# Retention queries decayed on GpSimd token tile by token tile, the group norm in two halves, and another turn count for the loads of w_out

## The chip, the cores and the metric

The kernel runs on one core of a Trainium2 chip. The metric is the device time of one execution in microseconds, and less is better. The core has five engines, each of which works through its own queue of instructions in order: TensorE (PE in the profile, with its weight loads as PEld), VectorE (DVE), ScalarE (ACT), GpSimd (POOL) and SyncE (SP, which here only issues transfers). An instruction waits at the head of its queue until the semaphores that it needs are set, and everything behind it on that engine waits too. TensorE has a granted clock: 1.00 in the profile is 2.4 GHz, 0.50 is 1.2 GHz.

## The reference

One transformer block over 1024 latent tokens and 256 context tokens, width 1024. The part that the change touches is the second head group, eight retention heads of width 64, in chunks of 128 tokens, run forward and backward:

```
inner = (q_c k_c^T) * decay_mat                       # within the chunk
o     = inner v_c + (q_c state) * q_decay             # q_decay: one factor per token of the chunk and head
state = state * chunk_decay + (k_c * k_decay)^T v_c   # k_decay: the same, for keys
ret   = group_norm(o_forward + o_backward) * silu(gate)   # mean and variance over the 64 of a head
out   = concat(attention, ret) @ w_out
```

The first head group is softmax attention (eight query heads, two key heads). A norm, a residual and a SwiGLU feed-forward follow. All data are fp32.

## The kernel before

The program has four stretches: the input projection, the mixing stage (attention and retention together), the output projection with `w_out`, and the feed-forward. The change lies in the mixing stage, from about 345 to 745 us of the trace.

**How the mixing stage is written.** Three Python generators are woven into one program. `attention()` walks over four pairs of heads `r`, two halves of 512 queries, ten key tiles and two heads: 160 steps, each of two score matmuls (L631, L632), an exponential on ACT (`p`, L633), four steps later two matmuls that weigh the values (`o`, L640), and the running sum `acc` of the exponentials on DVE or POOL (L688). `front(h)` finds the row maxima of the scores for head `h`: 24 score matmuls (L595), each of which DVE must read out with a maximum (`mx`, L596) before its PSUM bank is free. `retain(r)` does retention for a pair of heads:

- `U`: for each of ten token tiles the key tile is decayed on POOL (`decayed`, L737, tile `qk2`) and multiplied with the values (L751).
- The natural key and query tiles are transposed on TensorE to `kT`, `qT` (L768), copied from PSUM by ACT (L769).
- The decayed queries `q2T` are made from `qT` by DVE (forward direction) and POOL (backward direction), L774: per pair of heads four instructions on each engine, with the factors of the table `QD`.
- `ss`: the scan over the chunks, 16 small instructions on DVE (L782), and copies by ACT to `St`.
- `inner` (L799, and `im` on DVE, L802) and `outer` (L811, L813) for eight tiles; `outer` reads `q2T`.
- The group norm of `o` (L834 to L846) on DVE, ACT and POOL, then the gate product `rg` on POOL and a store to DRAM (`d_r`).

**What sets the order.** `weave` gives the next turn to the generator with the smallest share of its turns done; three weaves of 40 attention steps carry two fronts and a third of all retention turns each. What is left of the last pair's retention is written after the third weave, and the fourth weave carries the attention of the last pair and `load_w_out`: 16 halves of `w_out` tiles, each loaded by SP into one of two `raw` buffers, copied to `woh` by ACT (L125), and subtracted to `wol` by DVE (L126). A scheduler that builds the program then sets the order on each engine. The tiles `woh` lie in memory that retention has used.

Of the kernel before, what the change touches and what calls it, by code (L numbers as in the profile page):

```python
# [11 lines left out]
F32 = mybir.dt.float32  # L12
F32R = mybir.dt.float32r
AF = mybir.ActivationFunctionType
ALU = mybir.AluOpType
# [15 lines left out]
HR = 8  # L31
# [76 lines left out]
def hybrid_block(ctx: ExitStack, tc, x, c, cx, c_ctx, w_mod, b_mod, g_pre_mix, g_post_mix,  # L108
# [435 lines left out]
    lgq = bc.tile([P, 4, 2], F32, name="lgq")  # L544
    for j in range(2):
        for d in range(2):
            V.tensor_copy(out=lgq[j * HD:(j + 1) * HD, :, d],
                          in_=lg[j * HD:(j + 1) * HD, d * HR:(d + 1) * HR].rearrange("p (r j) -> p r j", j=2)[:, :, j])

# [10 lines left out]
    qs2, fr = {}, {}  # L560
# [8 lines left out]
    def front(h):  # L569
# [8 lines left out]
        V.tensor_tensor(out=q3[:, :, 0:HD], in0=qs, in1=f(q3[:, :, HD:2 * HD]), op=ALU.subtract)  # L578
# [30 lines left out]
    SKEW, V_ADDS, V_END, Q_ENG = 4, (2, 4, 6, 8), (2, 4, 6, 7, 8, 9), (V, G)  # L609
# [8 lines left out]
    def bank(tag):  # L618
        return pq.tile([P, 512], F32, tag=tag, name=tag)
# [97 lines left out]
    QD = rt.tile([P, 4, 2, P], F32, name="QD")  # L717

    def decay_matrices():
# [8 lines left out]
        for r in range(4):  # L728
            for d in range(2):
                S.activation(out=QD[:, r, d, :], in_=dcs[:, C_PR + d * P:C_PR + (d + 1) * P], func=AF.Exp, scale=lgq[:, r, d:d + 1])  # L730

    def retain(r):
        qn, kn, vn, gn = ret_load(r)

        def decayed(t):
            y = rt.tile([P, 2, 2, HD], F32, tag="qk2", name="qk2", bufs=3)
            G.tensor_tensor(out=y, in0=h3(kn[:, t, :]).unsqueeze(2).broadcast_to([P, 2, 2, HD]),  # L737
                            in1=dk[:, 1, 4 * r:4 * r + 4].rearrange("p (j d) -> p j d", d=2).unsqueeze(3).broadcast_to([P, 2, 2, HD]),
                            op=ALU.mult)
            return y  # L740
# [17 lines left out]
        if r == 0:  # L758
            decay_matrices()
# [3 lines left out]
        for nat, tr in ((kn, kT), (qn, qT)):  # L763
            for b in range(2):
# [5 lines left out]
                if nat is qn:  # L770
                    for j in range(2):
                        jsl = slice(j * HD, (j + 1) * HD)
                        for d in range(2):
# [60 lines left out]
        V.tensor_reduce(out=mu, in_=o4, axis=AX.X, op=ALU.add)  # L834
        V.tensor_scalar(out=mu, in0=mu, scalar1=1.0 / HD, scalar2=None, op0=ALU.mult)
        V.tensor_tensor(out=o4, in0=o4, in1=mu.unsqueeze(2).broadcast_to([P, nst, HD]), op=ALU.subtract)
        yield
        sq = rt.tile([P, nst, HD], F32, tag="kT", name="gsq")
        S.activation(out=sq, in_=o4, func=AF.Square)
        V.tensor_reduce(out=vr, in_=sq, axis=AX.X, op=ALU.add)  # L840
        V.tensor_scalar(out=vr, in0=vr, scalar1=1.0 / HD, scalar2=EPS, op0=ALU.mult, op1=ALU.add)
        for k in range(2):
            G.tensor_tensor(out=rs[:, k * 8:(k + 1) * 8], in0=vr[:, k * 8:(k + 1) * 8], in1=mhalf, op=ALU.pow)
        yield
        V.tensor_tensor(out=o4, in0=o4, in1=rs.unsqueeze(2).broadcast_to([P, nst, HD]), op=ALU.mult)
        G.tensor_tensor(out=gn, in0=o.rearrange("p t j e -> p t (j e)"), in1=gn, op=ALU.mult)  # L846
# [3 lines left out]
    N_FR, N_RT, N_AT = 13, 38, 40  # L850
# [29 lines left out]
    weave((islice(attend, N_AT), N_AT), (load_w_out(), 17))  # L880
# [401 lines left out]
```

## Time and profile before

| | |
|---|---|
| three runs | 1531.69, 1534.27, 1535.69 us; median 1534.27 |
| the profiled execution | 1534.52 us, of which the span from first to last instruction is 1532.7 |
| busy in the span | PE 1447.2, PEld 1083.8, DVE 866.4, ACT 518.6, POOL 501.7 us |
| mean granted clock of TensorE | 0.951 |
| mixing stage | some 400 us of the span |

Busy times are sums of the instructions of an engine. A matmul lasts about twice as long at clock 0.50, so a busy PE can still be a slow one. Idle time of an engine that nothing waits for costs nothing.

### The profile page before, as it was taken

Reading aid. Unit: us, or ns where it says so; the run is one execution under the profiler, and the core shown is the slowest. Engines: PE = TensorE matmul, PEld = TensorE weight load, DVE = VectorE, ACT = ScalarE, POOL = GpSimd, SP = SyncE. Lnnn points to the kernel's source line nnn. Section 1 sums busy time; section 2 is a strip of 40 time slices with the busy share of each in tenths; the row PEclk is TensorE's granted clock in tenths of the full one; section 3 lists DMA queues with packets and bytes.
Section 4 is the critical chain, followed back from the end, with each engine's and each line's share of the span. In section 5 each row is a group of like instructions: output and inputs, shape, how many; then the busy total and the mean of one; then the engine's idle time right before and its main releaser. Section 6 shows DMA issues by size and latency. Waiting matters only on the chain.

```text
span 1532.7 us, 19765 instructions
## 1 busy us (share of the span) xinstructions
PE 1447.2 (94%) x7290; PEld 1083.8 (71%) x7290; DVE 866.4 (57%) x1447; ACT 518.6 (34%) x1131; POOL 501.7 (33%) x382
## 2 busy tenths in 40 slices
PE   6999989998898989799899899999999999999997
PEld 2788867785454545454588678888888888888886
DVE  3667677445747676676455845444444444545445
ACT  3740221224344444545245623222222232113112
POOL 0112247303435273545003544444444441002003
PEclk9999999998676989899899999999999999999999
DMA  9456552314102020002433233222222224544662
GB/s 357 137 187 189 184 168 90 114 52 126 31 25 73 25 66 25 28 8 97 134 132 120 62 97 96 83 83 83 83 83 83 83 83 152 178 145 134 197 211 109
DMA packets 140623, 169.10 MB, mean 110 GB/s; under 512 B 8992, under 2 KB 90608, under 8 KB 140528
## 3 DMA queue, kind: packets, MB, share of 16 engines
q1 hardware_dynamic: 139680, 167.61, 33.9%
q8 instruction: 57, 0.93, 0.3%
q10 hardware_dynamic: 848, 0.25, 0.1%
q14 instruction: 38, 0.31, 0.1%
HBM read 132.17 MB, written 35.65 MB: 109 GB/s over the span
## 4 chain that ended last, share of the span: by engine, by line
PE 76%; DVE 11%; DMA 6%; issue 2%; ACT 2%; POOL 2%; SPq 0%; DVEq 0%; POOLq 0%; ACTq 0%
PE pb L131 45%; PE sb L131 14%; PE o L640 4%; PE sb L631 3%; PE sb L595 2%; DMA wm<-in_w_mod 2%; PE sb L632 2%; DVE q2T L774 1%; DMA rv<-d_p 1%; PE r L799 1%; DVE ss L782 1%; DVE mx L596 1%; PE sb L811 1%; PE r L751 1%; DVE wlo L126 1%
## 5 line engine op out<-in xcount | busy, mean ns | idle before, releaser
L131 PE MATMUL pb<-T,w 128*128 128x512 f32 x1320 | 316.7, 394 | 3.8 <-ACT w L125 2.0
L131 PEld LDWEIGHTS pb<-T,w 128*128 128x128 f32 x1320 | 247.8, 188 | 62.6 <-ACT w L125 2.6
L131 PE MATMUL pb<-whi,hT 128*128 128x512 f32 (+1 forms) x896 | 261.8, 373 | 5.2 <-ACT whi L125 4.6
L131 PEld LDWEIGHTS pb<-whi,hT 128*128 128x128 f32 x896 | 162.7, 191 | 39.3 <-ACT whi L125 5.5
L131 PE MATMUL pb<-wlo,hT 128*128 128x512 f32 (+1 forms) x448 | 165.7, 372 | 2.3 <-DVE wlo L126 2.2
L596 DVE TENSOR_REDUCE mx<-sb 128x1 f32<-128x512 f32 (+1 forms) x192 | 107.0, 596 | 62.9 <-PE sb L595 61.5
L126 DVE TENSOR_TENSOR w<-w1raw,w 128x512 fp32r<-128x512 f32 x152 | 123.3, 868 | 12.6 <-ACT w L125 12.6
L131 PE MATMUL sb<-B,w 128*128 128x512 f32 x504 | 124.8, 391 | 0.8 <-ACT u L1059 0.8
L633 ACT ACTIVATE p<-sb 128x512 f32<-128x512 f32 x160 | 92.3, 598 | 81.0 <-PE sb L632 77.0
L125 ACT CAST w<-w1raw 128x512 fp32r<-128x512 f32 x152 | 83.7, 619 | 94.1 <-POOL w1raw L1006 92.4
L688 POOL TENSOR_TENSOR acc<-acc,p 128x1024 f32<-128x1024 f32 x30 | 71.3, 2376 | 119.7 <-ACT p L633 109.1
L131 PEld LDWEIGHTS sb<-B,w 128*128 128x128 f32 x504 | 94.4, 188 | 22.1 <-ACT u L1059 1.3
L1138 POOL TENSOR_TENSOR g<-g,c 128x512 f32<-128x512 f32 x22 | 34.4, 1565 | 215.0 <-DVE c L1137 190.0
L131 PE MATMUL pb<-w,ah 128*128 128x512 f32 x328 | 101.5, 389 | 0.0
L640 PE MATMUL o<-p,VV 128*64 128x512 f32 x320 | 98.9, 684 | 2.8 <-ACT p L633 2.7
L131 PE MATMUL sb<-w,ah 128*128 128x512 f32 x328 | 101.4, 389 | 0.0
L131 PEld LDWEIGHTS pb<-wlo,hT 128*128 128x128 f32 x448 | 85.5, 191 | 18.7 <-DVE wlo L126 3.4
L176 POOL TENSOR_TENSOR ss<-ss,mhalf 128x1 f32<-128x1 f32 x26 | 14.7, 571 | 243.4 <-DVE ss L175 243.4
L131 PE MATMUL pb<-woh,rT 128*128 128x512 f32 x256 | 82.1, 401 | 0.6 <-DVE rT L125 0.6
L125 ACT CAST w<-raw 128x512 fp32r<-128x512 f32 x41 | 25.4, 624 | 168.5 <-PE pb L131 152.4
L125 DVE CAST ah<-ra 128x1024 fp32r<-128x1024 f32 x41 | 28.6, 698 | 88.4 <-PE pb L131 88.4
L631 PE MATMUL sb<-t,K 128*128 128x512 f32 x140 | 70.6, 504 | 7.7 <-DVE mx L596 5.8
(258 smaller groups left out, 2471.2 us busy)
## 6 DMA issues: line engine op xcount, KB each, us to landing
w1raw<-in_w_ffn_in SPq DMA_DIRECT2D x92, 256.0 KB, 3.4
ra<-d_a SPq DMA_DIRECT2D x41, 512.0 KB, 4.2
wm<-in_w_mod SPq DMA_DIRECT2D x64, 256.0 KB, 3.5
raw<-in_w_ffn_out SPq DMA_DIRECT2D x41, 256.0 KB, 3.9
d_p<-st SPq DMA_DIRECT2D x34, 256.0 KB, 2.0
wm<-in_w_mod SPq DMA_DIRECT2D x16, 512.0 KB, 6.8
raw<-in_w_in SPq DMA_DIRECT2D x32, 256.0 KB, 4.5
d_a<-g SPq DMA_DIRECT2D x22, 256.0 KB, 2.0
```

Of the source, the lines that this page charges most:

```text
L125: a = S.copy(out=hi, in_=src) if hi_eng is S else hi_eng.tensor_copy(out=hi, in_=src)
L126: return a, V.tensor_tensor(out=lo, in0=src, in1=f(hi), op=ALU.subtract)
L131: T.matmul(acc, lhsT=a, rhs=b, start=first and a is ah and b is bh, stop=last and a is al, skip_group_check=onto)
L595: T.matmul(sb[:, :n], lhsT=t1[:, t * P:(t + 1) * P], rhs=K1[:, kv, k0:k0 + n], start=True, stop=True)
L596: V.tensor_reduce(out=mx[:, t, j:j + 1], in_=sb[:, :n], axis=AX.X, op=ALU.max)
L631: T.matmul(sb, lhsT=K1[:, h // 4, ksl], rhs=t1[:, qsl], start=True, stop=False)
L632: T.matmul(sb, lhsT=K2[:, h // 4, ksl], rhs=t2[:, qsl], start=False, stop=True)
L633: S.activation(out=p[:, :, h % 2, :], in_=sb.rearrange("p (i n) -> p i n", n=P), func=AF.Exp)
L640: return T.matmul(st["o"][j * HD:(j + 1) * HD, :], lhsT=VV[kt][:, r // 2, :], rhs=p[:, :, j, :], start=(kt == 0), stop=(kt == AT - 1))
L688: eng.tensor_tensor(out=st["a"], in0=prev if kt == 1 else st["a"], in1=p, op=ALU.add)
L751: T.matmul(ub[d * HD:(d + 1) * HD, j * HD:(j + 1) * HD], lhsT=k2[t][:, j, d, :], rhs=vn[:, t, j * HD:(j + 1) * HD], start=True, stop=True)
L1138: G.tensor_tensor(out=g0, in0=g0, in1=c21, op=ALU.mult)
```

## The change

Four things change.

1. `q2T` is no longer made from `qT`. The natural query tile is decayed on POOL by the same helper as the keys (`decayed(t, qn, 0)`, one instruction for each of eight token tiles and pair of heads), transposed by TensorE (two transposes a tile), and copied from PSUM by ACT (one copy for two tiles). The tile `qk2` gets four buffers in place of three. The tables `QD` and `lgq` and the DVE and POOL products L774 go.
2. The DVE instructions of `decay_matrices` are queued behind the last query split of `front`.
3. The group norm is written in two halves of 8 of the 16 token tile and head columns, with a turn after each.
4. The turns of a retention pair are counted as 47 in place of 38, and those of `load_w_out` as 11 in place of 17.

```diff
-    lgq = bc.tile([P, 4, 2], F32, name="lgq")
...
-        V.tensor_tensor(out=q3[:, :, 0:HD], in0=qs, in1=f(q3[:, :, HD:2 * HD]), op=ALU.subtract)
+        hold["q"] = V.tensor_tensor(out=q3[:, :, 0:HD], in0=qs, in1=f(q3[:, :, HD:2 * HD]), op=ALU.subtract)
...
-        for r in range(4):
-            for d in range(2):
-                S.activation(out=QD[:, r, d, :], in_=dcs[:, C_PR + d * P:C_PR + (d + 1) * P], func=AF.Exp, scale=lgq[:, r, d:d + 1])
...
-        def decayed(t):
-            y = rt.tile([P, 2, 2, HD], F32, tag="qk2", name="qk2", bufs=3)
-            G.tensor_tensor(out=y, in0=h3(kn[:, t, :]).unsqueeze(2).broadcast_to([P, 2, 2, HD]),
-                            in1=dk[:, 1, 4 * r:4 * r + 4].rearrange("p (j d) -> p j d", d=2).unsqueeze(3).broadcast_to([P, 2, 2, HD]),
+        def decayed(t, src=kn, w=1):
+
+            y = rt.tile([P, 2, 2, HD], F32, tag="qk2", name="qk2", bufs=4)
+            G.tensor_tensor(out=y, in0=h3(src[:, t, :]).unsqueeze(2).broadcast_to([P, 2, 2, HD]),
+                            in1=dk[:, w, 4 * r:4 * r + 4].rearrange("p (j d) -> p j d", d=2).unsqueeze(3).broadcast_to([P, 2, 2, HD]),
...
         if r == 0:
-            decay_matrices()
+            with tc.issue_after(hold["q"].ins):
+                decay_matrices()
...
-                if nat is qn:
-                    for j in range(2):
-                        jsl = slice(j * HD, (j + 1) * HD)
-                        for d in range(2):
-                            Q_ENG[d].tensor_tensor(out=q2T[d * HD:(d + 1) * HD, j, bsl].rearrange("p (t n) -> p t n", n=P),
-                                            in0=qT[jsl, bsl].rearrange("p (t n) -> p t n", n=P),
-                                            in1=QD[jsl, r, d, :].unsqueeze(1).broadcast_to([HD, 4, P]), op=ALU.mult)
+                if nat is qn and b:
+                    q2 = [decayed(t, qn, 0) for t in range(2)]
                 yield
+
+        for t in range(0, LT, 2):
+            cur, q2 = q2, [decayed(t + 2 + i, qn, 0) for i in range(2)] if t + 2 < LT else None
+            tb = bank("r")
+            for i in range(2):
+                for j in range(2):
+                    T.transpose(out=tb[:, (2 * i + j) * P:(2 * i + j + 1) * P], in_=cur[i][:, j].rearrange("p d f -> p (d f)"),
+                                identity=ident)
+            S.copy(out=q2T[:, :, t * P:(t + 2) * P].rearrange("p j (i n) -> p i j n", n=P),
+                   in_=tb.rearrange("p (i j n) -> p i j n", i=2, n=P))
+            yield
...
+        halves = [slice(0, LT), slice(LT, nst)]
...
+        for h in halves:
+            V.tensor_tensor(out=o4[:, h], in0=o4[:, h], in1=mu[:, h].unsqueeze(2).broadcast_to([P, LT, HD]), op=ALU.subtract)
+            S.activation(out=sq[:, h], in_=o4[:, h], func=AF.Square)
+            yield
...
-    N_FR, N_RT, N_AT = 13, 38, 40
+    N_FR, N_RT, N_AT = 13, 47, 40
...
-    weave((islice(attend, N_AT), N_AT), (load_w_out(), 17))
+    weave((islice(attend, N_AT), N_AT), (load_w_out(), 11))
```

The queue of DVE in the first pair of heads, where the scan `ss` begins, before the change (`mx` are the row maxima, `im` the inner products with the decay matrix):

```order
L782 SCALAR_TENSOR_TENSOR ss<-ss,cd,U 128x64 x2
L596 TENSOR_REDUCE mx<-sb 128x1
L782 SCALAR_TENSOR_TENSOR ss<-ss,cd,U 128x64 x2
L596 TENSOR_REDUCE mx<-sb 128x1 x2
L782 SCALAR_TENSOR_TENSOR ss<-ss,cd,U 128x64 x2
L774 TENSOR_TENSOR q2T<-qT,QD 64x512 x2
L782 SCALAR_TENSOR_TENSOR ss<-ss,cd,U 128x64 x2
L688 TENSOR_TENSOR acc<-acc,p 128x1024
L802 TENSOR_TENSOR im<-r,DT 128x128
L596 TENSOR_REDUCE mx<-sb 128x1
L782 SCALAR_TENSOR_TENSOR ss<-ss,cd,U 128x64
L774 TENSOR_TENSOR q2T<-qT,QD 64x512 x2
```

The same place after the change:

```order
L779 SCALAR_TENSOR_TENSOR ss<-U,cd 128x64 x2
L590 TENSOR_REDUCE mx<-sb 128x1 x2
L779 SCALAR_TENSOR_TENSOR ss<-ss,cd,U 128x64 x9
L590 TENSOR_REDUCE mx<-sb 128x1
L779 SCALAR_TENSOR_TENSOR ss<-ss,cd,U 128x64
L590 TENSOR_REDUCE mx<-sb 128x1
L779 SCALAR_TENSOR_TENSOR ss<-ss,cd,U 128x64
L590 TENSOR_REDUCE mx<-sb 128x1
L682 TENSOR_TENSOR acc<-acc,p 128x1024
L779 SCALAR_TENSOR_TENSOR ss<-ss,cd,U 128x64 x2
L590 TENSOR_REDUCE mx<-sb 128x1 x2
```

The four query products are gone from between the maxima, and the scan has drawn together: nine of its instructions stand in one piece.

The queue of POOL at the end of `U` of the first pair, before (`rk` and `rq` are the natural key and query tiles):

```order
L737 TENSOR_TENSOR qk_3633<-rk,dk 128x256
L737 TENSOR_TENSOR qk_3659<-rk,dk 128x256
L688 TENSOR_TENSOR acc<-acc,p 128x1024
L774 TENSOR_TENSOR q2T<-qT,QD 64x512 x2
L737 TENSOR_TENSOR qk_4215<-rk,dk 128x256
L737 TENSOR_TENSOR qk_4217<-rk,dk 128x256
L737 TENSOR_TENSOR qk_4239<-rk,dk 128x256
L774 TENSOR_TENSOR q2T<-qT,QD 64x512 x2
```

After:

```order
L727 TENSOR_TENSOR qk_3622<-rk,dk 128x256
L727 TENSOR_TENSOR qk_3635<-rk,dk 128x256
L727 TENSOR_TENSOR qk_3737<-rq,dk 128x256
L727 TENSOR_TENSOR qk_3739<-rq,dk 128x256
L727 TENSOR_TENSOR qk_3750<-rq,dk 128x256
L727 TENSOR_TENSOR qk_3752<-rq,dk 128x256
L682 TENSOR_TENSOR acc<-acc,p 128x1024
L727 TENSOR_TENSOR qk_3765<-rq,dk 128x256
L727 TENSOR_TENSOR qk_3767<-rq,dk 128x256
L727 TENSOR_TENSOR qk_3782<-rq,dk 128x256
L727 TENSOR_TENSOR qk_3784<-rq,dk 128x256
```

Eight small query products stand in place of four larger ones, with one running sum between them.

The queue of ACT after the last pair's group norm, before (`gsq` is the square of the group norm, `rw` a row factor of the attention):

```order
L839 ACTIVATE gsq<-ro 128x1024
L633 ACTIVATE p<-sb 128x4x128 x4
L662 COPY rw<-rz 128x512
L633 ACTIVATE p<-sb 128x4x128 x12
L125 CAST woh_6304<-raw 128x512 x2
L633 ACTIVATE p<-sb 128x4x128 x4
L125 CAST woh_6339<-raw 128x512
```

After:

```order
L840 ACTIVATE gsq<-ro 128x512 x2
L599 CAST t_5517<-sb 65x512 x2
L627 ACTIVATE p<-sb 128x4x128 x6
L656 COPY rw<-rz 128x512
L627 ACTIVATE p<-sb 128x4x128 x6
L125 CAST woh_6446<-raw 128x512 x2
L627 ACTIVATE p<-sb 128x4x128 x4
L125 CAST woh_6519<-raw 128x512
```

The first cast of `w_out` stands behind 12 exponentials instead of 16. Further on, before the change four casts stand behind the last exponential of the attention, after it one.

## Rows read from the trace of the kernel before

**Rows 1.** Busy time by stretch (count), with clock: the mixing stage.
```profile
345.00:750.00 405.00, 359.90 (x2346) 205.53 (x2345) 259.08 (x434) 183.51 (x400) 173.46 (x108) 0.85 0.19 56
```
Columns: stretch, its length, busy time of PE, PEld, DVE, ACT and POOL, granted clock, DMA share, GB/s.

**Rows 2.** The same view, stretches in which PE has gaps.
```profile
390.00:405.00 15.00, 10.44 (x32) 5.51 (x31) 14.91 (x27) 4.70 (x11) 10.78 (x9) 0.71 0.20 58
470.00:490.00 20.00, 14.17 (x45) 8.19 (x45) 15.54 (x33) 8.82 (x20) 11.49 (x9) 0.62 0.32 96
560.00:575.00 15.00, 8.07 (x25) 4.27 (x24) 14.00 (x21) 3.19 (x6) 9.58 (x8) 0.73 0.06 16
625.00:640.00 15.00, 7.37 (x29) 4.14 (x30) 14.85 (x27) 3.85 (x9) 10.10 (x6) 0.73 0.24 70
...
730.00:745.00 15.00, 7.39 (x54) 5.25 (x52) 7.74 (x12) 4.38 (x8) 0.00 (x0) 0.64 0.50 147
```

**Rows 3.** The same view, stretches with a low clock.
```profile
395.00:440.00 45.00, 41.12 (x174) 20.84 (x174) 17.76 (x37) 12.75 (x26) 11.48 (x6) 0.54 0.00 1
475.00:505.00 30.00, 27.05 (x119) 13.95 (x118) 15.16 (x38) 12.49 (x26) 10.30 (x7) 0.55 0.12 34
565.00:580.00 15.00, 9.57 (x42) 5.32 (x42) 11.85 (x20) 3.60 (x7) 4.81 (x3) 0.66 0.00 0
630.00:650.00 20.00, 14.89 (x82) 8.69 (x82) 11.23 (x27) 9.38 (x20) 7.64 (x4) 0.66 0.09 27
```

**Rows 4.** Timeline of DVE (start, us, instructions, idle time before).
```profile
466.73 7.54 DVE L774 TENSOR_TENSOR q2T<-qT,QD 64x512 f32<-64x512 f32 x4
...
567.80 2.25 DVE L782 SCALAR_TENSOR_TENSOR ss<-ss,cd,U 128x64 f32<-128x64 f32 x1
...
570.30 0.27 DVE L782 SCALAR_TENSOR_TENSOR ss<-ss,cd,U 128x64 f32<-128x64 f32 x1
```

**Rows 5.** Timeline of PE: one wait, and the same work at either clock.
```profile
385.85 0.60 PE L768 MATMUL r<-ident,rk 128*128 128x128 f32 x4
...
388.78 1.08 PE L640 MATMUL o<-p,VV 128*64 128x512 f32 x4
...
405.92 1.98 PE L640 MATMUL o<-p,VV 128*64 128x512 f32 x4
...
570.43 0.79 PE L631 MATMUL sb<-t,K 128*128 128x512 f32 x1 [5.63 <-DVE mx L596]
```

**Rows 6.** Groups by line and form, 340 to 760 us (busy, mean ns of one).
```profile
L737 POOL TENSOR_TENSOR qk<-rk,dk 128x256 f32<-128x256 f32 x40 | 30.0, 773 | 92.8 <-DMA rk<-d_p 78.2 <-PE r L751 14.0 <-DVE vr L840 0.4
...
L774 POOL TENSOR_TENSOR q2T<-qT,QD 64x512 f32<-64x512 f32 x16 | 25.8, 1615 | 5.7 <-ACT qT L769 4.7
L774 DVE TENSOR_TENSOR q2T<-qT,QD 64x512 f32<-64x512 f32 x16 | 25.7, 1606 | 0.2
...
L769 ACT COPY qT<-r 128x512 f32<-128x512 f32 x8 | 4.6, 586 | 2.9 <-PE r L768 2.9
...
L841 DVE TENSOR_SCALAR vr<-vr 128x16 f32<-128x16 f32 x4 | 4.0, 1012 | 0.1
...
L730 ACT ACTIVATE QD<-dcs,lgq 128x128 f32<-128x128 f32 x8 | 2.7, 396 | 1.5 <-DMA dcs<-in_dec 1.5
```

**Rows 7.** Timeline of POOL.
```profile
365.53 1.75 POOL L737 TENSOR_TENSOR qk<-rk,dk 128x256 f32<-128x256 f32 x3 [78.17 <-DMA rk<-d_p]
...
567.29 2.67 POOL L688 TENSOR_TENSOR acc<-acc,p 128x1024 f32<-128x1024 f32 x1
```

**Rows 8.** Timeline of ACT, last pair.
```profile
681.09 1.06 ACT L839 ACTIVATE gsq<-ro 128x1024 f32<-128x1024 f32 x1
...
700.09 1.14 ACT L125 CAST woh<-raw 128x512 fp32r<-128x512 f32 x2 [1.38 <-DMA d_r<-rg]
```

**Rows 9.** Timeline of PE, from the attention's last sums to the output projection.
```profile
733.67 1.45 PE L657 MATMUL sb<-cst,acc 128*64 128x2 f32 x32 [2.32 <-DVE acc L688]
737.47 2.08 PE L668 MATMUL sb<-ident,rw 128*128 128x128 f32 x8 [2.36 <-ACT rw L662]
...
743.58 0.77 PE L131 MATMUL pb<-woh,rT 128*128 128x512 f32 x1 [0.64 <-DVE rT L125]
```

More of the change, by code (lines that the diff above doesn't have):

```diff
@@ L542, in hybrid_block @@
     S.activation(out=cd, in_=lgd, func=AF.Exp, scale=float(P))
-    lgq = bc.tile([P, 4, 2], F32, name="lgq")
-    for j in range(2):
-        for d in range(2):
-            V.tensor_copy(out=lgq[j * HD:(j + 1) * HD, :, d],
-                          in_=lg[j * HD:(j + 1) * HD, d * HR:(d + 1) * HR].rearrange("p (r j) -> p r j", j=2)[:, :, j])
     rawp = ph1.enter_context(tc.tile_pool(name="rawp", bufs=4))
@@ L558, in hybrid_block @@
     wks.close()
-    qs2, fr = {}, {}
+    qs2, fr, hold = {}, {}, {}
     def falloc(first, shape, dt, tag, bufs):
@@ L608, in hybrid_block @@
     N_FR = 15
-    SKEW, V_ADDS, V_END, Q_ENG = 4, (2, 4, 6, 8), (2, 4, 6, 7, 8, 9), (V, G)
+    SKEW, V_ADDS, V_END = 4, (2, 4, 6, 8), (2, 4, 6, 7, 8, 9)
     weave((project, 18), (chain(front(0), front(1)), 2 * N_FR))
@@ L715, in hybrid_block @@
     DT = rt.tile([P, HR, P], F32, name="DT")
-    QD = rt.tile([P, 4, 2, P], F32, name="QD")
     def decay_matrices():
@@ L833, in retain @@
         rs = rt.tile([P, nst], F32, tag="rsg", name="rsg")
-        V.tensor_reduce(out=mu, in_=o4, axis=AX.X, op=ALU.add)
+        halves = [slice(0, LT), slice(LT, nst)]
+        oh, gh = o.rearrange("p t j e -> p (t j) e"), gn.rearrange("p t (j e) -> p (t j) e", e=HD)
+        for h in halves:
+            V.tensor_reduce(out=mu[:, h], in_=o4[:, h], axis=AX.X, op=ALU.add)
+            yield
         V.tensor_scalar(out=mu, in0=mu, scalar1=1.0 / HD, scalar2=None, op0=ALU.mult)
-        V.tensor_tensor(out=o4, in0=o4, in1=mu.unsqueeze(2).broadcast_to([P, nst, HD]), op=ALU.subtract)
-        yield
         sq = rt.tile([P, nst, HD], F32, tag="kT", name="gsq")
[L839 to L846, printed above, removed]
+        for h in halves:
+            V.tensor_tensor(out=o4[:, h], in0=o4[:, h], in1=mu[:, h].unsqueeze(2).broadcast_to([P, LT, HD]), op=ALU.subtract)
+            S.activation(out=sq[:, h], in_=o4[:, h], func=AF.Square)
+            yield
+        for h in halves:
+            V.tensor_reduce(out=vr[:, h], in_=sq[:, h], axis=AX.X, op=ALU.add)
+            V.tensor_scalar(out=vr[:, h], in0=vr[:, h], scalar1=1.0 / HD, scalar2=EPS, op0=ALU.mult, op1=ALU.add)
+            G.tensor_tensor(out=rs[:, h], in0=vr[:, h], in1=mhalf, op=ALU.pow)
+            yield
+        for h in halves:
+            V.tensor_tensor(out=o4[:, h], in0=o4[:, h], in1=rs[:, h].unsqueeze(2).broadcast_to([P, LT, HD]), op=ALU.mult)
+            G.tensor_tensor(out=gh[:, h], in0=oh[:, h], in1=gh[:, h], op=ALU.mult)
+            yield
         nc.sync.dma_start(out=d_r[:, r * P:(r + 1) * P].rearrange("(t p) n -> p t n", p=P), in_=gn)
         yield
-    N_FR, N_RT, N_AT = 13, 38, 40
+    N_FR, N_RT, N_AT = 13, 47, 40
     attend = attention()
```

2 lines of the change are left out of this document (removed).

## The prediction

> **What bounds the kernel now.** I read first the busy times by stretch, then the gaps of TensorE in fine stretches, then the timelines of VectorE and GpSimd at each gap. The mixing stage takes 405 us from 345 to 750 us, in which PE is busy for 359.9, so 45.1 us are idle, and its mean clock is 0.85 [rows 1]. No other engine is near full there (DVE 259, ACT 184, POOL 173 us). So it is a stage of many short waits, and it matters where they fall.
>
> They fall in four bursts and at the end [rows 2]. The bursts are the stretches of 390, 470, 560 and 625 us, one for each pair of heads: idle PE is 15.00 less 10.44, or 4.56 us, then 5.83, 6.93 and 7.63, together 24.95 us or 6.24 a burst. In three of them DVE is at least 93% busy, in the second 78%. What DVE does there is the same each time: four query products, the scan, maxima and running sums. In the second burst the four products run in one piece of 7.54 us [rows 4]; no maximum can be taken meanwhile, no score bank comes free, and PE stops. At 570 us PE has waited 5.63 us for a maximum [rows 5].
>
> The wait is not all. After each burst the granted clock is at its lower level, 1.2 GHz, for a good while [rows 3]: clocks of 0.54, 0.55, 0.66 and 0.66 mean that 41.4, 27.0, 10.2 and 13.6 us were spent there (length times 1 minus the clock, over 0.5), 92 us in all. Of the 110 us of these stretches PE was idle in 17.4, so about 75 us of work ran at the lower level. Four weighing matmuls take 1.98 us there and 1.08 at 2.4 GHz [rows 5]; at the upper level 75 us would be 41, so the low clock costs about 34 us. What came before each fall of the clock is a burst's idle time.
>
> At the end of the stage PE is idle for 7.61 of 15 us [rows 2]: it waits 2.32 us for a running sum on DVE, 2.36 for a row factor on ACT, and starts the output projection at 743.58 us [rows 9]. Both engines have the last casts and differences of w_out in their queues there, and the first cast waited 1.38 us for the store of the last group norm, until 700.09 [rows 8].
>
> **The change, part by part.** *DVE's query products.* 16 instructions of 1606 ns go from DVE, 25.7 us [rows 6], or 6.4 a burst. That is the upper bound of what a burst can give, and more than its idle time. The lower bound comes from exclusion: a scan instruction that takes 0.27 us by itself took 2.25 us while a running sum of 2.67 us ran on POOL [rows 4, 7], so an instruction of DVE can be held for the length of one on POOL. POOL runs eight query products a burst from now on, at 0.58 us each at best (1.75 us for three [rows 7]), 4.7 us; if DVE's scan is held for all of that, a burst gains 1.7 us. I take 3.75, near the middle, since the maxima read PSUM and are not held: **-15 us** of idle (bounds -7 and -25). What is late next is the scan: nine of its instructions now stand in one piece, with the maxima behind them, for which PE's score banks wait.
>
> The Trainium skill, page "SBUF — State Buffer", section "Who interferes with whom", says that a VectorE instruction with two SBUF inputs and a GpSimd instruction that reads SBUF exclude each other for the whole instruction. The 2.25 us of that scan instruction agree. The rule speaks against moving the queries to GpSimd rather than away from both; by it the term would be -7 in place of -15, which is the third case below.
>
> *The clock.* With less idle time the clock falls later or not at all. Bounds 0 and -34. The two long stretches, after the first and second burst, hold 68 of the 92 us, and there nine and more scan instructions in a row may still stop PE. I take less than half: **-15 us**.
>
> *Transposes.* 64 more on PE (8 tiles, 2 heads, 4 pairs). Four take 0.60 us from start to end [rows 5], 0.15 each, 9.6 us in all; since groups overlap in the pipeline it is less, but some run at the lower clock. **+7** (5 to 15).
>
> *POOL.* 16 products of 1615 ns go (25.8 us); 32 of 773 come (24.7 us, by the mean of the key products, which have the same form) [rows 6]. The load is the same, the place is not: before, nobody but `outer` waited for them; now each pair of transposes waits on PE for its two tiles, and behind the waiting transpose stand the scores, the front's matmuls and the weighing. POOL is two tiles ahead by the order, and four buffers allow no more. **+4**, one us a burst (0 to 30; the upper end is the last case).
>
> *ACT.* 16 copies of 586 ns come, 9.4 us, and eight exponentials of 396 ns for `QD` go (3.2 us) [rows 6]. ACT is busy for 184 of 405 us [rows 1], so the copies are hidden in its idle time; uncovered they would cost 9.4. The exponentials stood ahead of the first scores, where PE also waits for loads: **-1** (0 to -3).
>
> *Group norm in halves.* The same elements in twice the instructions, whose fixed part costs DVE a little. The worst row is the small scaling of 1012 ns on 16 columns [rows 6]: if the halves take as long each, 4 us more. It lies on DVE, which is idle for 146 us of the stage: **+1** (0 to 4). The halves let ACT square one while DVE subtracts the other.
>
> *w_out.* The first cast stands behind 12 exponentials in place of 16. From the square at 681.09 to the cast at 700.09 us 16 exponentials went by [rows 8], 1.19 us each, so the cast comes to the head of ACT's queue 4.75 us sooner, while the store it waits for comes, with the halves, perhaps 2.5 us sooner. The wait grows from 1.38 to about 3.6 us, with all exponentials queued behind it; but four PSUM banks let PE go on for four steps, about 4.75 us, so **+1** (0 to 3.6). At the far end one cast instead of four follows the last exponential, so the running sum, the row factor and the load of the first mixed tile no longer stand behind w_out. Of the 7.61 us idle I keep 1.6 for the chain of sum, factor and transposes, and the first matmuls of the projection then run at the upper clock: **-8** (0 to -10). On SP more loads of w_out stand ahead of the store of the last pair's first half, which is read after all loads either way: 0. The natural queries are held until the last product, so the next pair's load of them, and in the second pair the values' load behind it on SP, wait longer; the values' buffer is in use until the last `outer` anyhow: 0.
>
> *Sum.* -15 - 15 + 7 + 4 - 1 + 1 + 1 - 8 = -26. The profiled execution took 1534.52 us (0.25 over the median of the three), which gives **1508.5 us**; as I see it between 1496 and 1523 if this is the case that holds.
>
> **The rivals.** *The clock stays up.* If the scan's pieces stop PE for no more than 1 us a burst, idle falls by 21, POOL costs nothing more, and 30 of the 34 us of clock come back: -21 - 30 + 7 + 0 - 1 + 1 + 1 - 8 = -51, **1483 us**. For it: the work in those stretches is far from full on any other engine (DVE 17.8 of 45 us [rows 3]). Against it: nine scan instructions in a row, each of which POOL can hold.
>
> *Exclusion eats the gain.* DVE's scan waits for POOL's products as it waited for its own; idle falls by 7, the clock does as before: -7 + 7 + 4 - 1 + 1 + 1 - 8 = -3, **1531.5 us**, no change. For it: the scan instruction of 2.25 us. Against it: POOL's load does not grow, and the products of DVE itself are gone.
>
> *Slower: PE waits for POOL's queue.* In the second pair's order a running sum and the two gate products stand ahead of the first query products, and another running sum in their midst. With running sums of 2.4 us (2.67 in [rows 7]), gate products of half a running sum each and eight products at 0.77, that is 13.6 us of POOL against four turns of PE, some 6 us, so 7.6 us of wait. If that holds in all four bursts, idle is 7.6 in place of 6.24 a burst, 5.4 us more, and at the present rate of clock loss to idle time (34 to 25) another 7.4: 5.4 + 7.4 + 7 - 1 + 1 + 1 - 8 = +13, **1547 us**. Since the other terms cancel, it decides from the point where a burst's wait passes 6.7 us. Against it: in the first pair the order puts four products ahead of the running sum, and the group norm's products come early where the halves work.
>
> **How the numbers follow.** The forecast 0.56, the clock 0.19, the exclusion 0.13, the queue of POOL 0.12. A measurement of this kernel tells about 0.3%, or 4.6 us, from no change. The first two are faster (0.75), the third the same (0.13), the last slower (0.12). The range 1484 to 1536 leaves out the far half of the clock's case and nearly all of the last, about 2 in 10; most of the chance lies on one side, and the forecast's own range stands above.
>
> **What would show it.** Right: in the four bursts idle PE falls to about 10 us, and the time at the lower clock after them to about half of 92 us; DVE's busy time in the stage falls by some 20 us; the output projection begins within 2 us of the last row factor. Wrong: transposes of query tiles that wait for POOL by more than 2 us; scan instructions of 1 us and more while POOL runs query products; a clock that falls just as early after the first burst; the first cast of w_out holding up exponentials so long that PE stands. The forecast fails most easily in the clock, since a burst that keeps 3 us of idle may still bring it down and then keeps most of its cost.

## The result, and the profile after

The changed kernel takes 1492.99 us (median of 4 runs, 1491.14 to 1495.43) against 1534.98 us before (4 runs, 1531.69 to 1537.06). The ratio is 0.9735 with a 95% interval of 0.9715 to 0.9755: faster by 42 us, where 26 were forecast. The profiled execution took 1494.64 us, 39.9 less than that of before. Four runs of later kernels that lie more than 1.5% above the fastest of their kernel are left out of the times below: one of the queries alone (1520.72 us), two with the query products on DVE (1524.83 and 1527.71) and one with the cast on ACT (2756).

The page of the changed kernel: span, busy times, and the granted clock in 40 slices.

```profile
span 1492.9 us, 19980 instructions
PE 1425.1 (95%) x7354; PEld 1074.7 (72%) x7354; DVE 849.8 (57%) x1447; ACT 525.8 (35%) x1143; POOL 496.5 (33%) x402
PEclk9999999999999989999999999999999999999999
```

PE is busy for 22 us less although it has 64 instructions more, so the same work ran at a higher clock. Nothing is gained outside the mixing stage: from the first projection matmul on, both kernels need the same time (743.58 to 1532.7 before, 704.11 to 1492.9 after: 789 us each). So I compare the stage from 345 us to that matmul (743.58 us before [rows 9], 704.11 us after). The columns are those of [rows 1]; first the kernel before, over that stretch:

```profile
345.00:743.58 398.58, 353.49 (x2327) 200.40 (x2326) 257.53 (x432) 183.51 (x400) 173.46 (x108) 0.85 0.18 53
```

Then the changed kernel: the stage, its four bursts, the group norm of the last pair (635), and the end.

```profile
345.00:704.11 359.11, 333.87 (x2403) 194.13 (x2402) 243.43 (x437) 189.85 (x411) 166.24 (x128) 0.96 0.20 59
...
390.00:405.00 15.00, 13.49 (x88) 8.07 (x86) 11.72 (x35) 11.15 (x23) 6.93 (x9) 1.00 0.28 80
440.00:465.00 25.00, 21.28 (x134) 12.53 (x130) 22.88 (x42) 15.17 (x35) 17.52 (x17) 1.00 0.32 90
520.00:540.00 20.00, 18.22 (x87) 9.66 (x86) 19.40 (x38) 10.91 (x23) 10.77 (x12) 0.92 0.42 123
590.00:605.00 15.00, 13.11 (x64) 7.63 (x64) 11.96 (x25) 10.33 (x22) 10.24 (x9) 0.89 0.24 72
635.00:650.00 15.00, 11.43 (x74) 7.30 (x72) 10.21 (x18) 7.58 (x15) 5.83 (x4) 0.89 0.00 0
...
690.00:704.11 14.11, 11.27 (x74) 6.06 (x71) 8.03 (x11) 6.80 (x13) 1.89 (x1) 0.88 0.38 110
```

The stage is 39.5 us shorter. Idle time (length less PE) falls from 45.1 to 25.2 us, and PE's busy time from 353.5 to 333.9. In the four bursts PE is idle for 1.51, 3.72, 1.78 and 1.89 us, 8.9 together, against 24.95 in [rows 2]; at the end for 2.84 against 7.61. The clock of 0.96 means that 29 us were spent at the lower level (359 times 0.04, over 0.5); 0.85 before means 120 us. After the first two bursts, where [rows 3] show 41 and 27 us at the lower level, it does not fall at all.

PE's largest waits in the stage before, all on DVE (waiting instruction, what it waits for, us in total, times, longest):

```profile
PE r L799 <- DVE im L802: 10.0, 4, 4.7
PE sb L631 <- DVE mx L596: 6.5, 3, 5.6
PE sb L595 <- DVE mx L596: 3.3, 2, 2.3
```

So DVE's queue held up PE in two ways of about the same size: through the maxima, 9.8 us, and through `im`, the product with the decay matrix that frees a PSUM bank for `inner`, 10.0 us. What is late now, in the same list:

```profile
PE sb L598 <- DVE q L593: 6.4, 4, 2.8
PE o L634 <- ACT p L627: 5.0, 4, 1.9
PE r L741 <- DMA rv<-d_p: 1.6, 2, 0.9
```

In the whole of that list the maxima come to 2.7 us. No transpose of a query tile stands in it as waiting for POOL; only their weight loads, which overlap other matmuls, wait for POOL, 2.3 us in five times. In POOL's own list it is POOL that waits, for the transposes to free its buffers:

```profile
POOL qk L727 <- PE r L770: 10.9, 3, 6.1
```

The timeline of PE at the third burst, where the clock falls, and at the end of the stage:

```profile
529.96 1.08 PE L634 MATMUL o<-p,VV 128*64 128x512 f32 x4
...
534.98 0.50 PE L625 MATMUL sb<-t,K 128*128 128x512 f32 x1 [1.25 <-DVE mx L590]
...
537.96 1.98 PE L634 MATMUL o<-p,VV 128*64 128x512 f32 x4
...
699.43 1.10 PE L651 MATMUL sb<-cst,acc 128*64 128x2 f32 x32 [0.38 <-DVE acc L682]
701.53 2.08 PE L662 MATMUL sb<-ident,rw 128*128 128x128 f32 x8 [1.00 <-ACT rw L656]
704.11 0.78 PE L131 MATMUL pb<-woh,rT 128*128 128x512 f32 x1
```

Four weighing matmuls take 1.98 us after the fall and 1.08 before it. At the end the two waits of 2.32 and 2.36 us [rows 9] are 0.38 and 1.00.

### The profile page after: what moved, and what is told of

It is laid out like the page before. It is cut to its first block, busy times and chain, and to the rows that moved or that the text cites. A ratio compares the mean times of both kernels' runs of the same rounds, so it can differ in the third digit from the quotient of the medians.

```text
span 1492.9 us, 19980 instructions
## 1 busy us (share of the span) xinstructions
PE 1425.1 (95%) x7354; PEld 1074.7 (72%) x7354; DVE 849.8 (57%) x1447; ACT 525.8 (35%) x1143; POOL 496.5 (33%) x402
## 4 chain that ended last, share of the span: by engine, by line
PE 80%; DVE 8%; DMA 6%; ACT 2%; issue 2%; POOL 1%; SPq 0%; DVEq 0%; POOLq 0%; ACTq 0%
PE pb L131 48%; PE sb L131 15%; PE o L634 4%; PE sb L625 3%; PE sb L589 2%; DMA wm<-in_w_mod 2%; PE sb L626 2%; DMA raw<-in_w_out 1%; DVE ss L779 1%; PE r L796 1%; DVE mx L590 1%; PE r L741 1%; PE sb L808 1%; DMA rv<-d_p 1%; DMA raw<-in_w_in 1%
## 5 line engine op out<-in xcount | busy, mean ns | idle before, releaser
L126 DVE TENSOR_TENSOR w<-w1raw,w 128x512 fp32r<-128x512 f32 x152 | 123.3, 867 | 15.7 <-ACT w L125 15.7
L634 PE MATMUL o<-p,VV 128*64 128x512 f32 x320 | 89.3, 637 | 5.1 <-ACT p L627 5.0
L319 POOL TENSOR_TENSOR st<-r,r 128x256 f32<-128x256 f32 (+1 forms) x32 | 42.3, 1323 | 90.0 <-DVE r L318 64.2
```

Of the source, the lines that this page charges most:

```text
L126: return a, V.tensor_tensor(out=lo, in0=src, in1=f(hi), op=ALU.subtract)
L319: G.tensor_tensor(out=dst, in0=t1, in1=t2, op=ALU.add)
L634: return T.matmul(st["o"][j * HD:(j + 1) * HD, :], lhsT=VV[kt][:, r // 2, :], rhs=p[:, :, j, :], start=(kt == 0), stop=(kt == AT - 1))
```

## The experiments

My theory was that TensorE's stops come from DVE having no room between the maxima, and that most of their price is the low clock behind them. The rivals were that GpSimd's products would hold DVE as much as DVE's own had (exclusion), and that PE would wait for GpSimd's queue. All times are medians; "stage" is the stretch from 345 us to the first projection matmul in the profiled run, with idle PE, busy PE and clock.

| kernel | us (range, runs) | ratio to before (95%) | stage | idle | busy | clock |
|---|---|---|---|---|---|---|
| before | see above | 1 | 398.6 | 45.1 | 353.5 | 0.85 |
| loads' pace alone | 1533.32 (1528.68-1535.95, 10) | 1.000 (0.998-1.002) | 397.4 | 44.9 | 352.5 | 0.86 |
| halves alone | 1527.93 (1525.28-1534.59, 10) | 0.9964 (0.9943-0.9984) | 391.5 | 42.1 | 349.4 | 0.88 |
| queries alone | 1499.62 (1495.94-1507.22, 3) | 0.9766 (0.9710-0.9822) | 369.3 | 26.9 | 342.4 | 0.92 |
| after, old pace | 1492.67 (1490.05-1502.10, 5) | 0.9768 (0.9743-0.9793) | 357.2 | 22.8 | 334.4 | 0.95 |
| after, no halves | 1505.94 (1500.08-1509.05, 5) | 0.9839 (0.9819-0.9860) | 368.0 | 26.3 | 341.7 | 0.92 |
| after, no hold | 1495.66 (1491.46-1497.70, 4) | 0.9749 (0.9724-0.9773) | 355.6 | 24.6 | 331.0 | 0.96 |
| after, once more | 1493.01 (1491.70-1500.19, 5) | 0.9749 (0.9724-0.9774) | 357.1 | 24.2 | 333.0 | 0.95 |

The kernel before gave 1534.04 us beside the three single parts, 1529.11 beside the old pace and the kernel without halves, 1534.07 beside the last two; so ratios are compared, not times.

**The queries alone.** The changed kernel with the group norm, the turn counts (42 turns a pair, 17 for the loads) and the order of the decay matrices as before.

> The kernel before with the new way of the queries alone (decayed on GpSimd, transposed, copied; 42 turns a pair); group norm, w_out turns and the place of the decay matrices as before. Theory (the query products on VectorE stood ahead of the maxima in four bursts, PE stopped, and the clock fell): most of the gain of 42 us is here, 1500 to 1508 us, with some 70 us less at the lower clock after the bursts. Rival (the gain is made of several small parts and a luckier order): 1515 us or more.

Ratio 0.9766: about 36 of the 42 us. In the stage, idle time falls by 18.2 us and PE's busy time by 11.1, although the transposes (10.6 us) are in it, so the clock gives some 21.7; the time at the lower level falls from 120 to 59 us, where some 70 less were expected. By this ratio the other parts have 6 us to share, but the kernel without halves below gives them more.

**The halves alone.** The kernel before with

```diff
-    N_FR, N_RT, N_AT = 13, 38, 40
+    N_FR, N_RT, N_AT = 13, 44, 40
```

and the group norm of the change.

> The kernel before with the group norm in halves alone (44 turns a pair). Theory: no change beyond 5 us, 1530 to 1540 us, since the four bursts keep their query products on VectorE. Rival (the finer group norm lets the maxima through): 1520 us or less.

Ratio 0.9964, some 5.5 us: just over the 5 us that the theory allowed, and far from the rival's 14 or more. The end of the stage is already near that of the changed kernel (timeline of PE): from the last sums to the projection it takes 5.8 us, 4.7 in the changed kernel and 9.9 before [rows 9].

```profile
730.66 1.10 PE L657 MATMUL sb<-cst,acc 128*64 128x2 f32 x32 [0.38 <-DVE acc L688]
...
736.50 0.77 PE L131 MATMUL pb<-woh,rT 128*128 128x512 f32 x1 [0.86 <-DVE rT L125]
```

**The pace alone.** The kernel before with `(load_w_out(), 11)` in place of 17.

> The kernel before with 11 turns in place of 17 for the loads of w_out, nothing else. Theory: up to 8 us at the end of the mixing stage, 1526 to 1535 us, if the end waits for the queues of casts; the rival, that the chain of two raw buffers from the last group norm's store on sets the end, gives no change, 1535 us.

Ratio 1.000. The first and the last cast of w_out on ACT in this kernel:

```profile
699.21 1.14 ACT L125 CAST woh<-raw 128x512 fp32r<-128x512 f32 x2 [1.38 <-DMA d_r<-rg]
736.43 0.62 ACT L125 CAST woh<-raw 128x512 fp32r<-128x512 f32 x1
```

They lie 37.2 us apart; in the kernel before 37.5 (700.09 [rows 8] and 737.63), with the halves alone 37.1, in the changed kernel 36.7, though there the first cast does not wait for the store:

```profile
661.12 1.13 ACT L125 CAST woh<-raw 128x512 fp32r<-128x512 f32 x2
...
697.83 0.61 ACT L125 CAST woh<-raw 128x512 fp32r<-128x512 f32 x1
```

The turn count does not set this distance. Nine of the casts in the changed kernel wait for the load of their `raw` tile, 11.3 us in all (list of ACT's waits), so the two buffers are the likely pace; no run with more of them was made. What can be won is an earlier first cast, and it waits 1.38 us for the store of the last group norm here as it did before.

**The changed kernel with the old pace, and without the halves.** First `(load_w_out(), 17)`, then the old group norm with 42 turns a pair.

> The changed kernel with the old turn count of the w_out loads (17 in place of 11). Theory one: once the stage is short, the late loads, casts and differences of w_out again stand at its end. In the kernel with the queries alone, which has the old count, PE waited 3.12 us for the last running sum and 1.89 us before the first projection matmul; that is 4 to 5 us back, 1497 to 1498 us. Theory two: the two raw buffers set the end whatever the count, as in the old kernel with the new count alone (ratio 1.000): 1493 us, no difference over 2 us.

> The changed kernel with the group norm in one piece, as before, and 42 turns a pair in place of 47. Theory one: the halves are worth what they were alone, some 5.5 us (0.9964): 1498.5 us. Theory two: they are worth the whole distance from the kernel with the queries alone, 1503 us, because long pieces of 128x1024 now stand among the maxima of a stage whose clock is otherwise up. Theory three: with the query products gone DVE has room for long pieces: 1493 us.

With the old pace 0.9768 against 0.9735 and 0.9749 for the changed kernel: the intervals overlap, and the end is the same (the last sum is again waited for 0.38 us). Theory two holds, the pace is worth nothing that these runs can tell. Without the halves 0.9839, 14 to 16 us worse and past the 5.5 that they are worth alone, so theory two again. The stage has 1 us more idle time than the changed kernel's, but PE is busy for 7.8 us longer with the same work, at clock 0.92 (windows of this kernel):

```profile
345.00:712.95 367.95, 341.65 (x2375) 196.57 (x2374) 237.83 (x415) 189.33 (x406) 166.36 (x124) 0.92 0.20 58
```

And PE waits 2.8 us for the last running sum, with the new pace in place (list of its waits):

```profile
PE sb L651 <- DVE acc L682: 2.8, 1, 2.8
```

The group norm, not the pace, eased the end. This kernel differs from the queries alone only in the pace and in the hold of the decay matrices, and the two profiled stages are alike (368.0 and 369.3 us), yet the ratios are 0.9839 and 0.9766. So the share of the queries by themselves is known only as 25 to 36 us of the 42, and what the halves and the rest add as 6 to 17.

**DVE's products put back.** To the changed kernel 16 products of 64x512 on DVE are added at the old place; nothing reads them.

```diff
+                if nat is qn:
+                    for j in range(2):
+                        jsl = slice(j * HD, (j + 1) * HD)
+                        junk = rt.tile([P, 512], F32, tag="junk", name="junk")
+                        V.tensor_tensor(out=junk[0:HD, :]..., in0=qT[jsl, bsl]..., in1=DT[jsl, r, :]..., op=ALU.mult)
```

> The changed kernel with four products of 64x512 a pair put back on VectorE at the old place, into a tile that nobody reads; they are extra work and leave the output alone. Theory: the bursts stop PE again and the clock falls again, 25 us or more back, 1515 to 1535 us, with PE waiting for maxima. Rival (what counted was GpSimd's or the scheduler's order, not VectorE's time): 1500 us or less.

1517.14 us (1508.72 to 1526.63, 4 runs), ratio 0.9894 (0.9830 to 0.9957): 24 us above the changed kernel. The stage in this kernel (windows), and the added products (groups):

```profile
345.00:730.74 385.74, 357.92 (x2399) 204.28 (x2398) 251.58 (x452) 191.18 (x412) 172.39 (x128) 0.90 0.19 55
```

```profile
L765 DVE TENSOR_TENSOR junk<-qT,DT 64x512 f32<-64x512 f32 x16 | 15.7, 982 | 0.3
```

The stage is 26.6 us longer than the changed kernel's. Idle time accounts for only 2.6 of it; PE has the same instructions and is busy for 24.0 us longer, at clock 0.90 in place of 0.96. So in these two executions 15.7 us of DVE work, which cost PE 2.6 us of waiting, cost 24 us of clock. The time is the theory's, but its sign hardly came: PE waits for maxima for 3.7 us, against 2.7 in the changed kernel. That DVE's products at this place bring the loss back is shown; that the clock falls through longer stops of PE is not.

**Whose time, and the exclusion.** Three kernels move the query work: the changed kernel with the 32 products of query tiles on DVE; the kernel before with all products of `q2T` on GpSimd; and the changed kernel with each query product on GpSimd done twice into the same tile.

```diff
-            G.tensor_tensor(out=y, in0=h3(src[:, t, :])...
+            (G if src is kn else V).tensor_tensor(out=y, in0=h3(src[:, t, :])...
```

> The changed kernel with the 32 query products of token tiles on DVE in place of GpSimd; transposes and copies as in the changed kernel. A product of 128x512 takes 0.69 us on DVE, so one of 128x256 should take some 0.4: 13 us of DVE, half of the 25.7 that went, in place of 23 us of GpSimd. Theory one: DVE's time is what counts, whoever else runs; half of it back costs 4 to 12 us against the changed kernel, 1497 to 1505 us. Theory two, exclusion: DVE loses more to GpSimd's query products than the 13 us; without them the scans run at 0.27 us and the time is that of the changed kernel or less, 1486 to 1494 us.

Five runs, 1499.20 to 1519.40 us, median 1506.30, 13 us above the changed kernel beside it; by the ratio, 0.9869 (0.9829 to 0.9909) against 0.9749, it is 18. Theory one holds, and it costs a little more than its 4 to 12 us. The groups of DVE here, with the scan for comparison:

```profile
L779 DVE SCALAR_TENSOR_TENSOR ss<-ss,cd,U 128x64 f32<-128x64 f32 x56 | 24.4, 466 | 0.0
L727 DVE TENSOR_TENSOR qk<-rq,dk 128x256 f32<-128x256 f32 x32 | 19.0, 616 | 6.5 <-PE r L741 3.5 <-POOL qk L727 3.0
```

In the changed kernel the same 56 scan instructions take 461 ns each:

```profile
L779 DVE SCALAR_TENSOR_TENSOR ss<-ss,cd,U 128x64 f32<-128x64 f32 x56 | 23.0, 461 | 0.0
```

So the query tiles on GpSimd do not make the scan longer in the mean: 461 ns with them, 466 without. They do hold it, but briefly. In the changed kernel's second burst eleven scan instructions run beside four query products (timelines of DVE and POOL):

```profile
452.05 3.46 DVE L779 SCALAR_TENSOR_TENSOR ss<-ss,cd,U 128x64 f32<-128x64 f32 x11
...
451.74 2.32 POOL L727 TENSOR_TENSOR qk<-rq,dk 128x256 f32<-128x256 f32 x4 [0.82 <-PE r L770]
```

That is 0.31 us each, and in the whole stage no scan instruction beside a query product takes over 0.65 us; the long ones, up to 2.4 us, lie beside running sums.

```diff
-    SKEW, V_ADDS, V_END, Q_ENG = 4, (2, 4, 6, 8), (2, 4, 6, 7, 8, 9), (V, G)
+    SKEW, V_ADDS, V_END, Q_ENG = 4, (2, 4, 6, 8), (2, 4, 6, 7, 8, 9), (G, G)
```

> The kernel before with all four query products of a step on GpSimd, none on DVE: 16 of 1.6 us change the engine, 25.7 us, and nothing else does (no transposes, no copies). Theory one: what counts is that DVE has room between the maxima; then this gives most of what the queries alone gave, ratio 0.975 to 0.985, 1495 to 1510 us. Theory two, exclusion: eight products of 1.6 us a pair on GpSimd hold DVE's scan for as long as its own products did; ratio 0.995 to 1.005. Theory three: the products come too late for the instructions that read them, since GpSimd needs 12.9 us for them a pair; then the waits move to the output matmuls and the ratio is over 1.005.

1509.08 us (1504.20 to 1519.21, 4 runs), ratio 0.9848 (0.9814 to 0.9882): theory one, at its edge. Taking the products off DVE, and nothing else, gives 23 us without any transposes. But exclusion takes a part here, which the groups show (DVE's scan, in this kernel and in the one before), then the timelines of DVE and POOL in the first burst, then that burst's window, all from its slowest run (1519.21 us):

```profile
L782 DVE SCALAR_TENSOR_TENSOR ss<-ss,cd,U 128x64 f32<-128x64 f32 x56 | 37.7, 726 | 0.0
```

In the kernel before:

```profile
L782 DVE SCALAR_TENSOR_TENSOR ss<-ss,cd,U 128x64 f32<-128x64 f32 x56 | 22.3, 447 | 0.1
```

```profile
394.23 4.61 DVE L782 SCALAR_TENSOR_TENSOR ss<-ss,cd,U 128x64 f32<-128x64 f32 x8
...
392.01 5.42 POOL L774 TENSOR_TENSOR q2T<-qT,QD 64x512 f32<-64x512 f32 x4
```

```profile
390.00:405.00 15.00, 10.67 (x35) 5.11 (x34) 15.00 (x21) 6.39 (x14) 14.50 (x12) 0.72 0.28 80
```

Eight scan instructions take 4.61 us beside the large products, where nine took 1.84 us in the changed kernel. The scan's mean rises from 447 to 726 ns, 15 us in all, and the first burst is as before: PE 10.67 of 15 us and clock 0.72, against 10.44 and 0.71 [rows 2]. The rule of the Trainium skill that the prediction weighed (page "SBUF — State Buffer", section "Who interferes with whom") agrees with these rows: the scan with its two inputs in SBUF and the products shut each other out.

```diff
+            for _ in range(2 if src is qn else 1):
                 G.tensor_tensor(out=y, in0=h3(src[:, t, :])...
```

> The changed kernel with each query product on GpSimd done twice into the same tile, 32 instructions of 0.71 us more, 23 us of GpSimd in all or 5.7 us a pair; the output is the same. Theory one: the transposes do not wait for GpSimd, which itself stands 10.9 us for PE to free tiles, so most of the second products lie in that slack: 2 to 8 us more, 1495 to 1501 us. Theory two, my rival of the queue: the transposes are just in time, so a doubling shows in full and brings the clock down with it: 20 to 45 us more, 1513 to 1538 us, with waits of PE for the decayed tiles of over 2 us a pair.

1504.75 us (1499.57 to 1507.55, 4 runs), ratio 0.9835 (0.9816 to 0.9854): 12 us over the changed kernel, by the ratios 15, between the two ranges. The profiled run lies at 1499.57, with 5.3 us more idle time in a stage of the same busy time (windows, then PE's weight loads in the list of waits):

```profile
345.00:709.12 364.12, 333.60 (x2402) 195.27 (x2400) 244.35 (x436) 190.24 (x411) 185.83 (x160) 0.97 0.20 58
```

```profile
PEld r L771 <- POOL qk L728: 2.8, 4, 0.8
```

The transposes' weight loads wait for GpSimd by 0.8 us at most, 2.8 us in all against 2.3 in the changed kernel, even with twice the query products on it. The rival of the queue needed over 2 us a pair; it falls. What grows is PE's wait for maxima, from 2.7 to 5.8 us, which fits a DVE that is held more often; no run takes that apart.

**The cast of the row maxima on ACT.** It is what PE waits for longest in the changed kernel.

```diff
-        V.tensor_copy(out=q3[:, :, 2 * HD:2 * HD + 1], in_=nm.unsqueeze(2))
+        S.copy(out=q3[:, :, 2 * HD:2 * HD + 1], in_=nm.unsqueeze(2))
```

> The changed kernel with the cast of the row maxima (128x8) on ACT in place of DVE. PE's largest wait in the changed kernel is for this cast, 7.8 us in all, and one such cast took 2.17 us in place of 0.17 beside a running sum on GpSimd. Theory one: the cast leaves DVE's queue and GpSimd's hold on it, half or more of that wait goes and some clock comes back: 3 to 7 us less, 1486 to 1490 us. Theory two: the last maximum and the maximum over the three parts, which stay on DVE ahead of the cast, are what is late: 0 to 2 us less, 1491 to 1493 us.

Four runs, 1488.61 to 1499.63 us, median 1495.8, ratio 0.9775 (0.9750 to 0.9800). No gain: its time lies some 3 us above the range of theory two, its waits are those of theory one (list of PE's waits, then windows).

```profile
PE sb L598 <- ACT q L593: 2.7, 2, 1.7
```

```profile
345.00:703.14 358.14, 336.82 (x2402) 195.08 (x2401) 237.01 (x429) 190.14 (x418) 166.37 (x128) 0.95 0.20 59
```

The wait falls from 6.4 to 2.7 us and the stage's idle time by 3.9 us, but PE is busy for 2.9 us longer with the same work, at clock 0.95 in place of 0.96, and the changed kernel's own repeat has 0.95 as well.

**No hold, and the changed kernel once more.** First `decay_matrices()` without the hold behind the last query split, then the changed kernel unchanged.

> The changed kernel without the hold of the decay matrices' DVE instructions behind the last query split. 16 instructions of 0.3 to 0.7 us, 7.7 us in all, then stand ahead of the split at 368 us, for which the front's transposes wait. Theory one: that wait grows to several us at the start of the stage, where the clock is at its lower level already: 3 to 8 us more, 1496 to 1501 us. Theory two: the start waits for loads and for the first split anyway: 1492 to 1494 us, no difference over 2 us.

> The changed kernel itself once more, as the measure for the other three beside it and for how far one kernel's runs lie apart. Both theories expect 1491 to 1496 us and a ratio of 0.972 to 0.977; a spread of over 5 us from run to run, with the granted clock lower in the longer runs, would say that the clock is what varies.

Both 0.9749, theory two: the hold is worth nothing that can be measured. The repeat gives the gain a second time, and its five runs lie 8.5 us apart. That is more than 5, but the longest run (1500.19 us, clock 0.978) has no lower a clock than the next (1498.40, 0.975), so the clock alone does not explain this spread. No version here can be called better than the changed kernel: old pace, no hold and cast on ACT all lie within 0.3% of its repeat.

## Why the prediction was right, and where its sizes were off

Direction and place held, and so did the cause, DVE's query products. The sum came out 13.9 us too small a gain (1494.64 for the profiled run against 1508.5): just below the forecast's own range, which began at 1496, inside the wider one, and 11.6 us from the rival in which the clock stays up (1483). Measured in the stage: idle time -19.8, transposes +10.6, and what is left of PE's busy time, -19.6 less 10.6, is by this reckoning the clock, -30.2. Together -39.4, against -39.9 for the whole execution. The clock's term is off by 15.2 us, more than the whole error; that the other errors nearly cancel is luck.

- *Idle in the bursts, -15.* Measured -16.0 (24.95 to 8.9). Right in size, and the sign to look for (about 10 us) came. I had told it as maxima that come late; by the list of waits before, as much was `im` in the same queue. The exclusion that I had put against it exists, but costs little here: the query products are short, and hold a scan instruction for 0.65 us at most. In the first burst POOL even stood 6.07 us for PE while nine scan instructions went by at full pace (timelines of DVE and POOL of the changed kernel):

```profile
391.12 1.84 DVE L779 SCALAR_TENSOR_TENSOR ss<-ss,cd,U 128x64 f32<-128x64 f32 x9
...
396.06 2.34 POOL L727 TENSOR_TENSOR qk<-rq,dk 128x256 f32<-128x256 f32 x4 [6.07 <-PE r L770]
```

- *The clock, -15.* This is the step that was mis-sized: -30.2, near the bound of -34. I took less than half, since scan instructions in a row might still stop PE in the first two bursts. PE stops there for 1.51 and 3.72 us in pieces of at most 1.17 us, and the clock stays at its upper level. The bound came from 92 us at the lower level after the bursts, while the stage as a whole had 120, so it was no bound for the stage. The rival in which the clock stays up had this term right, though its condition, stops of no more than 1 us a burst, did not come; it expected 5 us too much of the bursts and had the same 7 us for the transposes.
- *Transposes, +7.* Measured 10.6: 64 of 278 ns each, less the time in which they overlap each other (busy us, mean ns, idle time of PE before them):

```profile
L770 PE MATMUL r<-ident,qk 128*128 128x128 f32 x64 | 10.6, 278 | 0.0
```

- *POOL, +4.* Nothing that shows: PE is not idle before the transposes (the 0.0 in that line), and POOL waits for PE to free its four buffers. Twice the products cost some 5 to 15 us. The sum in the rival of the queue gives 13.4 us by its own terms, not 13.6; it changes nothing.
- *The far end of w_out, -8.* The gain is there, -4.8 (7.61 to 2.84), but the cause was put wrongly. It is the halves, which bring it by themselves and without which it goes; one and a half times the pace gives nothing, alone or with the rest. The first cast does not wait for the store in the changed kernel, so the +1 for that wait fell away too. The projection begins 2.6 us after the last row factor is written (701.48), not within 2.
- *ACT -1, halves +1.* Too small to be told apart; what is left of idle time outside bursts and end is +1.0 us. The halves as a whole were costed at +1 beside the end's -8, and are worth 5.5 us alone and about 14 with the queries, most of it clock and the end.
- *DVE's busy time, some 20 less.* It fell by 14.1 us (257.5 to 243.4), though 25.7 us of products went: the halves make up 5.6 of the rest (237.8 without them, 243.4 with them), and what the other 6 are is not shown.

What stays open is when the clock falls and how long it stays down. The kernel with DVE's products put back had 27.8 us of idle time and 77 us at the lower level (385.74 times 0.10, over 0.5), the changed kernel 25.2 and 29, and the one with GpSimd's products twice had the most idle time, 30.5 us, and only 22 at the lower level. So the sum of the idle time does not decide it. And in the kernel before the clock stays at 0.50 through 30 us in which PE has no gap at all (windows):

```profile
405.00:435.00 30.00, 30.00 (x135) 15.12 (x133) 7.22 (x18) 9.45 (x19) 4.22 (x3) 0.50 0.00 1
```

How the stops lie among the matmuls may decide, but no run here isolates that. What the runs show is that the low clock goes with the products on DVE: it goes when they go and comes back with them. The prediction's step from less idle time to a clock that falls less is not shown. More `raw` buffers, which would test what paces w_out, were not tried.

## What to carry to other kernels

When a stage has many short stops of TensorE and a clock below full in the same stretches, cost the time at the lower level beside the idle time: here the clock gave one and a half times as much as the waits, and one edit that changed idle time by 2.6 us moved the end of the stage by 26.6. Take work off the engine that reads the score banks out, and where it goes to GpSimd, choose short pieces: products of 64x512 (1.26 us at the fastest) raised the scan from 447 to 726 ns in the mean, token tiles (0.58 at the fastest) left it at 461. The turn count of a stream of loads was worth nothing here, where two buffers are the likely pace; look for what lets its first step begin.

## What the runs showed of the hardware

**One program, 20 us of spread, in the order of the clock.** The five runs of the kernel with query products on DVE, by granted clock: 0.976 1499.20 us, 0.973 1504.02, 0.972 1506.30, 0.965 1513.66, 0.962 1519.40. The order is the same in both columns. From the first to the last the time at the lower level, twice (1 less clock) times the time, goes from 72 to 115 us, and half of the 43 is 22 us; 20.2 were measured. So what the clock does differs from run to run of such a kernel, and its profile shows only one of the runs (here the fastest); the kernel before, in the 12 runs beside it, spread over 10.6 us.

**GpSimd's running sums hold even tiny DVE instructions.** In the changed kernel, a cast of 128x8 and a scaling of 128x16 beside a running sum on POOL (timelines of DVE and of POOL):

```profile
461.07 2.17 DVE L593 CAST q<-nm 128x8 fp32r<-128x8 f32 x1
...
642.48 1.73 DVE L836 TENSOR_SCALAR mu<-mu 128x16 f32<-128x16 f32 x1
...
460.87 2.35 POOL L682 TENSOR_TENSOR acc<-acc,p 128x1024 f32<-128x1024 f32 x1 [1.44 <-ACT p L627]
...
641.83 2.35 POOL L682 TENSOR_TENSOR acc<-acc,p 128x1024 f32<-128x1024 f32 x1 [6.21 <-ACT p L627]
```

The cast's median in the stage is 0.17 us, and both end within 0.1 us of the running sum. These have one input in SBUF, where the scan has two. The Trainium skill, page "SBUF — State Buffer", section "Who interferes with whom", says that casts and scalings can take the port pair that DVE shares with GpSimd in a two-port mode, too; these rows agree.

**The old products were dear because POOL was at work beside them.** A product of 64x512 takes 0.69 us on DVE when no instruction runs on POOL, as one of those put back shows (timeline of DVE; POOL's products end at 456.19 and begin again at 457.90):

```profile
456.50 0.69 DVE L765 TENSOR_TENSOR junk<-qT,DT 64x512 f32<-64x512 f32 x1
```

Before, the mean was 1606 ns [rows 6]. The four that took 7.54 us in the second burst [rows 4] ran beside a gate product and two of POOL's own query products (timeline of POOL):

```profile
467.53 2.82 POOL L846 TENSOR_TENSOR rg<-ro,rg 128x1024 f32<-128x1024 f32 x1
470.43 3.28 POOL L774 TENSOR_TENSOR q2T<-qT,QD 64x512 f32<-64x512 f32 x2
```

I had read those 1606 ns as the instruction's own length; more than half was, by these rows, waiting for POOL.
